# Moving a decoder layer's parameter rows from two queues to a third, and adding two warm-up products

## The chip, the cores and the metric

One Trainium2 chip; the kernel runs on one of its cores. The metric is device time of one execution, in microseconds, median of the runs shown. Smaller is better.

## The reference

One decoder layer on 256 tokens of width 1024. A normalised input `h` goes through one wide projection; two branches (a recurrent mixer and block attention) use its columns, are gated, merged and projected back; then a gated MLP with a short convolution follows.

```python
h = rms_norm(x, norm1_g)                       # x: 256 x 1024
proj = h @ w_in                                # w_in: 1024 x 5408
z = proj[..., :1824]                           # recurrent branch
z = z + rwkv_mu * (shift_right(z) - z)         # per-channel mixing
y_a = rwkv7_time_mix(z, w_decay_up, decay_bias, w_aaa_up, aaa_bias, w_gate_up,
                     k_k, k_a, r_k, ln_g, ln_b)
y_b = moba_attention(rope(q), rope(k), v)      # rope reads `positions`
x = x + (sigmoid(ga) * (y_a @ w_branch_a) + sigmoid(gb) * (y_b @ w_branch_b)) @ w_out
x = x + conv_ffn(rms_norm(x, norm2_g), w_ffn_up, ffn_conv_w, ffn_conv_b, w_ffn_down)
```

What the change touches are the small per-channel vectors: `rwkv_mu`, `decay_bias`, `aaa_bias`, `k_k`, `k_a`, `r_k`, `ln_g`, `ln_b`, and `positions`. None of them is over 8 KB.

## The kernel before, in words

**Products.** Every large product is made in three parts, to keep float32 accuracy with a faster number type: a weight block of 512 KB (`raw`) is fetched, ScalarE (ACT) rounds it to `whi`, VectorE (DVE) takes the rest, `wlo = raw - whi`, and TensorE (PE) multiplies `whi` with the high and the low half of the input (`hh`, `hl`) and `wlo` with the high half. 124 blocks go through these steps; a ring of four `raw` buffers, and four more at the start, let the transfers run ahead.

**The start.** `first_steps()` is written out by hand, engine by engine (a manual schedule: each engine takes its instructions in the order of the code). It holds what happens before the first ordinary block:
- PE first multiplies a tile of ones with itself (`keep_warm`, 8 products of 128x512 in bf16), whose results nobody reads.
- `turn(t, k)` transposes the 16 pieces of `x` on PE (`L427`): first four of the second token half, then the row of `norm1_g` (`p0`, `L438`), then the eight of the first half (`xn`, already scaled by DVE), then the last four.
- ACT and DVE make `hh` (`high`, `L446`) and `hl` (`low`, `L449`) of them.
- `first(0, ..)` and `first(1, ..)` are the products of the first two weight blocks (`L489`), 24 each, into the bank `idle`. Between them stands `params_turned()` (`L149`): PE transposes `p1`, a tile of 43 rows in which all the small vectors of the recurrent branch stand one below the other. DVE then copies the result (`L153`). `p1` is filled by nine small transfers.
- Behind the second block come the transposition of the second half's scale (`L508`) and 32 products with the narrow columns `wtr` (`L515`). Then the ordinary blocks begin (`L304`, `L306`, `L309`).

**The queues.** Transfers are issued by SP (the sync queue), by ACT, and by POOL (GpSimd); each engine issues in its own order. `loads` is a list of the small transfers in this order: the nine rows of `p1`, two of `wdu`, then `wgu`, four of `wgt`, two of `gqk`, `posi` (the positions), three of `p2`. `first_steps()` takes them from the list: ACT issues the first two (`rwkv_mu`, 14 rows and one), SP the two of `wdu`, POOL the other seven rows of `p1` and `posi`.

**Completion counters.** The tile layer gives each transfer of SP and ACT one of eight counters, in rotation, in the order of the code. A transfer that takes a counter in use waits on its queue until the earlier transfer of that counter has landed, and with it waits all that stands behind it on that queue. POOL's transfers have counters of their own. Such waits stand as `DMAHW0` to `DMAHW7` in the lists below.

Of the kernel before, what the change touches and what calls it, by code (L numbers as in the profile page):

```python
# [36 lines left out]
def body(tc, x, positions, norm1_g, w_in, rwkv_mu, w_decay_up, decay_bias, w_aaa_up,  # L37
         aaa_bias, w_gate_up, k_k, k_a, r_k, ln_g, ln_b, q_norm_g, k_norm_g, w_branch_a,
         w_branch_b, w_out, norm2_g, w_up, conv_w, conv_b, w_down, out):
    nc = tc.nc  # L40
    act, dve, pool, pe = nc.scalar, nc.vector, nc.gpsimd, nc.tensor
    ctx = ExitStack()
    with ctx:
# [128 lines left out]
        loads, at_ = [], 0  # L172
# [19 lines left out]
        loads += [(p2[0:66], conv_w[0].rearrange("w (n c) -> (w n) c", c=128)), (p2[66:88], rows(conv_b, 22)),  # L192
                  (p2[88:96], rows(norm2_g, 8))]

        def small_loads(n):
            for _ in range(n):
                nc.gpsimd.dma_start(*loads.pop(0))

        last_exp, last_tanh = [], []
        trig = cst.tile([128, 2, 2, HALF], F32, name="trig")  # L200
        rot = cst.tile([128, 2, 2, 2, 2, HALF], F32, name="rot")
# [43 lines left out]
        def load_next(first=False, early=False):  # L245
            if skipped[0]:
                skipped[0] -= 1
            elif queue:
                ap = queue.pop(0)
                k, c = ap.shape[1], ap.shape[2]  # L250
                raw = b4("raw", (128, 1024)) if early else wp.tile([128, 1024], F32, name="raw", tag="raw", bufs=NRAW)
                rv = raw[:, :k * c].rearrange("p (k c) -> p k c", k=k)
                for ks in ((slice(0, 2), slice(2, 4)) if first else (slice(0, k),)):
                    nc.sync.dma_start(rv[:, ks], ap[:, ks])
                raws.append((raw, k, c))
# [120 lines left out]
        wtr = b2("wtr", [128, 8, 32])  # L376

        def first_steps():
            for _ in range(2):
                nc.scalar.dma_start(*loads.pop(0))  # L380
            for i in range(2 * NRAW):
                load_next(i == 0, early=i >= NRAW)
                if i == 2:
                    nc.sync.dma_start(wtr, win[:, :, 1792:1824])
                if i == 3:
                    for _ in range(2):
                        nc.sync.dma_start(*loads.pop(7))
            skipped[0] = NRAW
            dve.memset(ones, 1.0)
            dve.memset(eps1[:, 0:1], NORM_EPS)  # L390
# [3 lines left out]
            def keep_warm(n):  # L394
                for _ in range(n):
                    pe.matmul(p, ones[:, 0:128], ones, start=True, stop=True)

            keep_warm(8)
            pool.iota(jp, pattern=[[1, 128]], base=0, channel_multiplier=-1)
            pool.tensor_scalar(ident, jp, 0.0, None, op0=OP.is_equal)  # L400
            for q in range(2):
                pool.iota(jl[64 * q:64 * q + 64], pattern=[[0, 2], [1, 64]], base=0, channel_multiplier=-1)
            small_loads(7)
            nc.gpsimd.dma_start(*loads.pop(7))
            act.activation(warm, eps1[:, 0:1], AF.Sqrt)
            ss = sb.tile([128, 2, 2], F32, name="ss1")
            bk = [b("xt") for b in (chp, chp, chp, atp, atp, acc, acc)]
# [17 lines left out]
            def turn(t, k):  # L425
                src = x_sb[t][:, k * 128:k * 128 + 128] if t else xn[k // 4][:, k % 4 * 128:k % 4 * 128 + 128]
                pe.transpose(at(k)[:, t * 128:t * 128 + 128], src, ident)  # L427
# [9 lines left out]
            pt = bk[5][:, 256:264]  # L437
            pe.transpose(pt, p0, ident[:8, :8])  # L438
            dve.tensor_copy(par[:, 0:8], pt)
            for k in (0, 1, 2, 3, 4, 6, 7, 5):  # L440
                turn(0, k)
            for k in (4, 6, 7, 5):
# [2 lines left out]
            def high(k):  # L445
                act.activation(hh[:, k], at(k), AF.Copy, scale=col(G1 + k))  # L446
# [17 lines left out]

            for cs in quarters:
                pool.tensor_copy(w[0][1][:, cs], w[0][0][:, cs])
            for k in (0, 1, 2, 3, 4, 6, 7, 5):
                high(k)
            for cs in halves_:
# [61 lines left out]
        with tc.manual_schedule(engines={E.PE, E.Activation, E.DVE, E.Pool}):  # L531
            xwa, xg, tls = first_steps()
# [825 lines left out]
        for j in range(11):  # L1358
# [20 lines left out]
            for m in range(2):  # L1379
                n = 2 * j + m  # L1380
# [68 lines left out]
```

## Time and profile before

| what | value |
|---|---|
| median of 3 runs | 404.61 us (404.5 to 404.91) |
| the profiled execution | 404.9 us, its span 403.1 us |
| PE busy | 398.0 us, 99% of the span |
| ACT, DVE, POOL busy | 234.7, 321.8, 44.4 us |
| DMA | 70.36 MB, mean 175 GB/s |

The span goes from the first to the last instruction that the profiler saw; 1.8 us of the execution lie around it. PE, ACT, DVE, POOL are the compute engines, PEld is PE's weight load, SP issues transfers. A row of the timeline gives start and duration in us, engine, line, operation, output and inputs with their shapes, the count, and in brackets how long the engine had been idle before and what ended that.

### The profile page before, as it was taken

The page shows a single profiled execution, that of the slowest core. Times are in us where ns is not written, and L with a number is a line of the kernel's source. Part 1 is how long each engine was busy: PE and PEld are TensorE (multiplying, and loading weights), DVE is VectorE, ACT ScalarE, POOL GpSimd, SP SyncE. Part 2 cuts the span into 40 slices and gives each one's busy share as a digit, 9 for nine tenths or more (in the row PEclk, how much of TensorE's full clock was granted, in tenths as well). Part 3 has the DMA queues.
Part 4 walks back from the last instruction along what each step waited for, and adds up shares of the span by engine and source line. Part 5 has one row for each costly group of instructions (what it writes and reads, how often), then busy time and mean ns, then how long its engine had stood idle before and what let it go on. Part 6 is the DMA issues. An engine that isn't in the chain of part 4 may idle for free.

```text
span 403.1 us, 8318 instructions
## 1 busy us (share of the span) xinstructions
PE 398.0 (99%) x3282; PEld 347.9 (86%) x3282; DVE 321.8 (80%) x554; ACT 234.7 (58%) x396; POOL 44.4 (11%) x76
## 2 busy tenths in 40 slices
PE   8999999999999999999999999999999999999996
PEld 5899899888899898999888888888888888888885
DVE  4798999989667897688876897977869779687694
ACT  6899766366555795454564764545546446355450
POOL 7600505213410011100000000000000000000000
PEclk9999999999999999999999999999999999999999
DMA  7983556746844335536664657565665665656612
GB/s 246 299 269 82 138 157 210 205 132 146 224 124 142 106 88 155 167 123 206 201 179 141 210 167 232 165 206 182 198 202 167 209 193 171 209 180 198 195 54 106
DMA packets 60194, 70.36 MB, mean 175 GB/s; under 512 B 7608, under 2 KB 50506, under 8 KB 60154
## 3 DMA queue, kind: packets, MB, share of 16 engines
q1 hardware_dynamic: 59222, 69.40, 57.0%
q0 software_dynamic: 880, 0.41, 0.6%
q8 instruction: 26, 0.43, 0.5%
q14 instruction: 14, 0.11, 0.1%
q10 hardware_dynamic: 52, 0.01, 0.0%
HBM read 68.37 MB, written 1.44 MB: 173 GB/s over the span
## 4 chain that ended last, share of the span: by engine, by line
PE 98%; DMA 1%; SPq 0%; DVE 0%; issue 0%
PE acc L1330 20%; PE acc L1335 10%; PE acc L304 9%; PE acc L306 8%; PE acc L309 8%; PE acc L325 5%; PE acc L329 5%; PE acc L326 5%; PE f L1352 5%; PE f L1350 5%; PE f L1354 5%; PE idle L489 2%; PE pgr L715 1%; PE xt L427 1%; DMA x<-in_x_dram 1%; PE ppt L1155 1%
## 5 line engine op out<-in xcount | busy, mean ns | idle before, releaser
L266 ACT CAST whi<-raw 128x1024 fp32r<-128x1024 f32 x122 | 127.8, 1051 | 111.6 <-PE acc L1330 41.2
L276 DVE TENSOR_TENSOR wlo<-raw,whi 128x1024 fp32r<-128x1024 f32 x122 | 148.3, 1218 | 37.0 <-PE acc L1335 14.0
L1330 PE MATMUL acc<-hx,whi 128*128 128x512 f32 x352 | 89.5, 395 | 0.0
L1330 PEld LDWEIGHTS acc<-hx,whi 128*128 128x128 f32 x352 | 63.4, 188 | 12.4
L304 PE MATMUL acc<-hx,whi 128*128 128x256 f32 x224 | 56.3, 287 | 0.0
L306 PE MATMUL acc<-hx,whi 128*128 128x256 f32 x224 | 54.1, 278 | 0.0
L1335 PEld LDWEIGHTS acc<-hx,wlo 128*128 128x128 f32 x352 | 46.8, 188 | 4.0
L1335 PE MATMUL acc<-hx,wlo 128*128 128x256 f32 x352 | 47.3, 277 | 0.0
L304 PEld LDWEIGHTS acc<-hx,whi 128*128 128x128 f32 x224 | 42.1, 188 | 2.5 <-issue 1.4
L306 PEld LDWEIGHTS acc<-hx,whi 128*128 128x128 f32 x224 | 42.1, 188 | 0.1
L309 PE MATMUL acc<-hx,wlo 128*128 128x256 f32 x224 | 34.6, 276 | 0.0
L1352 PE MATMUL f<-whi,hb 128*128 128x512 f32 x80 | 31.2, 390 | 0.0
L1354 PE MATMUL f<-wlo,hb 128*128 128x512 f32 x80 | 31.2, 390 | 0.0
L1350 PE MATMUL f<-whi,hb 128*128 128x512 f32 x80 | 31.2, 389 | 0.0
L309 PEld LDWEIGHTS acc<-hx,wlo 128*128 128x128 f32 x224 | 29.6, 188 | 0.0
L1340 DVE TENSOR_REDUCE an<-acc 128x256 f32<-128x512 f32 x22 | 14.2, 686 | 9.4 <-PE acc L1335 9.3
L325 PE MATMUL acc<-whi,hx 128*128 128x512 f32 x48 | 19.4, 405 | 0.0
L326 PE MATMUL acc<-whi,hx 128*128 128x512 f32 x48 | 18.8, 391 | 0.0
L1354 PEld LDWEIGHTS f<-wlo,hb 128*128 128x128 f32 x80 | 15.0, 188 | 3.2
L1352 PEld LDWEIGHTS f<-whi,hb 128*128 128x128 f32 x80 | 15.0, 188 | 2.8
L1350 PEld LDWEIGHTS f<-whi,hb 128*128 128x128 f32 x80 | 15.0, 188 | 2.8
L329 PE MATMUL acc<-wlo,hx 128*128 128x512 f32 x48 | 14.9, 392 | 0.0
(341 smaller groups left out, 635.1 us busy)
## 6 DMA issues: line engine op xcount, KB each, us to landing
raw<-in_w_ffn_up_dram SPq DMA_DIRECT2D x44, 512.0 KB, 4.4
raw<-in_w_in_dram SPq DMA_DIRECT2D x41, 512.0 KB, 4.1
raw<-in_w_ffn_down_dram SPq DMA_DIRECT2D x22, 512.0 KB, 3.3
raw<-in_w_out_dram SPq DMA_DIRECT2D x8, 512.0 KB, 3.9
x<-in_x_dram SPq DMA_DIRECT2D x8, 256.0 KB, 4.2
raw<-in_w_branch_b_dram SPq DMA_DIRECT2D x4, 512.0 KB, 4.6
raw<-in_w_branch_a_dram SPq DMA_DIRECT2D x4, 512.0 KB, 3.5
out_dram<-o SPq DMA_DIRECT2D x3, 256.0 KB
```

Source lines behind the costliest of these rows:

```text
L266: act.copy(hi[:, :k * c], raw[:, :k * c])
L276: eng.tensor_tensor(lo[:, :n], raw[:, :n], hi[:, :n].bitcast(F32), op=OP.subtract)
L304: pe.matmul(om, wh[:, k, ms], xh[:, k0 + k], start=k0 + k + m == 0, stop=False, skip_group_check=True)
L306: pe.matmul(om, wh[:, k, ms], xl[:, k0 + k], start=False, stop=False, skip_group_check=True)
L309: pe.matmul(om, wl[:, k, ms], xh[:, k0 + k], start=False, stop=k0 + k == nk - 1 and m == n - 1, skip_group_check=True)
L325: pe.matmul(ps_[t], xh[:, K, ts], wh[:, k], start=K == 0, stop=False)
L326: pe.matmul(ps_[t], xl[:, K, ts], wh[:, k], start=False, stop=False)
L1330: pe.matmul(ps_[m], wh[:, k, m * 128:m * 128 + 128], hx[:, k0 + k].rearrange("p a s -> p (a s)"), start=k0 + k == 0, stop=False, skip_grou ...
L1335: pe.matmul(ps_[m][:, 0:S], wl[:, k, m * 128:m * 128 + 128], hh[:, k0 + k], start=False, stop=k0 + k == 7, skip_group_check=True)
L1350: pe.matmul(fin[f], hb[:, 0, i, ts], wh[:, 0, cs], start=st, stop=False, skip_group_check=f == 3)
L1352: pe.matmul(fin[f], hb[:, 1, i, ts], wh[:, 0, cs], start=False, stop=False, skip_group_check=f == 3)
L1354: pe.matmul(fin[f], hb[:, 0, i, ts], wl[:, 0, cs], start=False, stop=False, skip_group_check=f == 3)
```

## The change

All nine rows of `p1` are issued by SP, behind the third weight block and ahead of `wtr`; `posi` is issued by POOL later, behind its four rounding copies of the first weight block; there is one more `keep_warm` product at the start, and one behind the transposition of `p0`.

```diff
-        def small_loads(n):
-            for _ in range(n):
-                nc.gpsimd.dma_start(*loads.pop(0))
...
         def first_steps():
-            for _ in range(2):
-                nc.scalar.dma_start(*loads.pop(0))
             for i in range(2 * NRAW):
                 load_next(i == 0, early=i >= NRAW)
                 if i == 2:
+                    for _ in range(9):
+                        nc.sync.dma_start(*loads.pop(0))
                     nc.sync.dma_start(wtr, win[:, :, 1792:1824])
                 if i == 3:
                     for _ in range(2):
-                        nc.sync.dma_start(*loads.pop(7))
+                        nc.sync.dma_start(*loads.pop(0))
...
-            keep_warm(8)
+            keep_warm(9)
...
-            small_loads(7)
-            nc.gpsimd.dma_start(*loads.pop(7))
...
             dve.tensor_copy(par[:, 0:8], pt)
+            keep_warm(1)
...
                 pool.tensor_copy(w[0][1][:, cs], w[0][0][:, cs])
+            nc.gpsimd.dma_start(*loads.pop(7))
```

SP's list before, from the second half of the first weight block on (`raw` are weight blocks, the first in two halves; `128x2x256` is half a block):

```order
L254 DMA raw<-in_w_in_dram 128x2x256 [waits DMAHW0_49]
L254 DMA raw<-in_w_in_dram 128x4x256 [waits DMAHW1_49]
L254 DMA raw<-in_w_in_dram 128x4x256 [waits DMAHW2_49]
L384 DMA wtr<-in_w_in_dram 128x8x32 [waits DMAHW3_49]
L254 DMA raw<-in_w_in_dram 128x4x256 [waits DMAHW4_49]
L387 DMA wdu<-in_w_decay_up_dram 64x512 [waits DMAHW5_49]
L387 DMA wdu<-in_w_aaa_up_dram 64x512 [waits DMAHW6_49]
L254 DMA raw<-in_w_in_dram 128x4x256 [waits DMAHW7_49]
```

SP's list now, from the third weight block to the fourth (`p` is `p1`):

```order
L250 DMA raw<-in_w_in_dram 128x4x256 [waits DMAHW0_49]
L379 DMA p_70<-in_rwkv_mu_dram 14x128 [waits DMAHW1_49]
L379 DMA p_70<-in_rwkv_mu_dram 1x4x32 [waits DMAHW2_49]
L379 DMA p_70<-in_decay_bias_dram 4x128 [waits DMAHW3_49]
L379 DMA p_70<-in_aaa_bias_dram 4x128 [waits DMAHW4_49]
L379 DMA p_70<-in_rwkv_k_k_dram 4x128 [waits DMAHW5_49]
L379 DMA p_70<-in_rwkv_k_a_dram 4x128 [waits DMAHW6_49]
L379 DMA p_70<-in_rwkv_r_k_dram 4x128 [waits DMAHW7_49]
L379 DMA p_70<-in_rwkv_ln_g_dram 4x128 [waits DMAHW0_49]
L379 DMA p_70<-in_rwkv_ln_b_dram 4x128 [waits DMAHW1_49]
L380 DMA wtr<-in_w_in_dram 128x8x32 [waits DMAHW2_49]
L250 DMA raw<-in_w_in_dram 128x4x256 [waits DMAHW3_49]
```

The nine rows stand between the third block and `wtr`, and since ACT issues only `p0` now, the counters have moved: 0 is held by `p0` and then by the third block, 1 to 4 by the four pieces of `x`, 5 and 6 by the halves of the first block, 7 by the second block. So the row of `r_k` waits for the second block to land, that of `ln_g` for the third, and that of `ln_b` for the first row of `rwkv_mu`. `wtr`, the fourth block and all behind them come after the last row.

On PE, the stretch from the first transpositions to the first weight block, now:

```order
L421 MATMUL xt<-ident,x 128x128 x4
L432 MATMUL xt<-ident,p_69 128x8
L392 LDWEIGHTS ones
L392 MATMUL idle<-ones 128x512
L421 MATMUL xt<-ident,xn_168 128x128 x4
L421 MATMUL xt<-ident,xn_169 128x128 x4
```

The pair of `ones` is new there; before, the transpositions of `xn` followed that of `p0` (`p_69`) at once. The transposition of `p1` keeps its place between the first and the second weight block on PE, and waits for all nine rows. Line numbers of the new kernel are 4 to 6 lower than before from line 195 on. Apart from these places the order on PE, DVE, ACT and POOL is the same as before; on SP one of the four small `wgt` transfers goes ahead of a later weight block instead of behind it.

## The prediction

> **What bounds the kernel.** First the page: busy times, then the chain that ended last.
>
> ```profile
> PE 398.0 (99%) x3282; PEld 347.9 (86%) x3282; DVE 321.8 (80%) x554; ACT 234.7 (58%) x396; POOL 44.4 (11%) x76
> PE 98%; DMA 1%; SPq 0%; DVE 0%; issue 0%
> ```
>
> PE is busy almost without a break, and 98% of the chain lies on it. So what PE loses or gains at the start it keeps: little later slack takes it back. Everything that the change touches is used in the first 25 us, so PE's timeline there comes next.
>
> ```profile
> 1.46 3.60 PE L396 MATMUL idle<-ones 128*128 128x512 bf16 x8 [1.46 <-DVE eps L391]
> 5.50 1.09 PE L427 MATMUL xt<-ident,x 128*128 128x128 f32 x4 [0.45 <-DMA x<-in_x_dram]
> 6.52 0.27 PE L438 MATMUL xt<-ident,p 8*128 8x8 f32 x1
> 6.72 1.97 PE L427 MATMUL xt<-ident,xn 128*128 128x128 f32 x8
> 8.48 1.06 PE L427 MATMUL xt<-ident,x 128*128 128x128 f32 x4
> 9.20 2.86 PE L489 MATMUL idle<-hx,whi 128*128 128x256 f32 x16
> 11.89 1.07 PE L489 MATMUL idle<-hx,wlo 128*128 128x256 f32 x8
> 12.89 0.26 PE L149 MATMUL pt<-ident,p 43*128 43x43 f32 x1
> 13.08 2.10 PE L489 MATMUL idle<-hx,whi 128*128 128x256 f32 x16
> 15.02 1.07 PE L489 MATMUL idle<-hx,wlo 128*128 128x256 f32 x8
> 15.93 0.27 PE L508 MATMUL pt<-ident,rx 128*128 128x128 f32 x1
> 16.13 1.93 PE L515 MATMUL tl<-hx,wtr 128*32 128x256 f32 x32
> 17.99 0.38 PE L304 MATMUL acc<-hx,whi 128*128 128x256 f32 x1
> ```
>
> PE takes these in this order. The point to watch is L149 at 12.89, the transposition of `p1`: 24 products of the first block stand ahead of it, 24 of the second behind it. If `p1` is late, PE stands. Next, PE's pace: the same product, first and second block (columns of durations: minimum, median, maximum in ns).
>
> ```profile
> L489 PE MATMUL idle<-hx,whi x7: 392/415/562, 9.2 to 10.6; 128*128 128x256 f32 x7
> L489 PE MATMUL idle<-hx,whi x16: 276/276/384, 13.1 to 14.9; 128*128 128x256 f32 x16
> ```
>
> The median falls from 415 to 276 ns, though the granted clock stands at 1.00 in every stretch (third number from the end in the rows of stretches below): until about 10.7 PE ran slowly. The warm-up products aim at that.
>
> **The rows of `p1`: what they leave.** POOL's last row and its landing (last number of the second line, us after issue), and an idle ACT:
>
> ```profile
> 5.51 0.52 POOL L197 DMA_DIRECT2D p<-in_rwkv_ln_b_dram  x1
> ...
> p<-in_rwkv_ln_b_dram POOLq DMA_DIRECT2D x1, 2.0 KB, 6.1
> ...
> 1.39 1.06 ACTq L380 DMA_DIRECT2D p<-in_rwkv_mu_dram  x2
> ...
> 8.11 1.43 POOL L466 CAST whi<-raw 128x256 fp32r<-128x256 f32 x4 [1.31 <-DMA raw<-in_w_in_dram]
> ```
>
> Today `p1` is complete at 5.51 + 6.1 = 11.6, ahead of 12.89. POOL gains its issue time, but then waits for the first weight block until 8.11 as today; ACT gains 1.06, but PE's first transposition waits for `x` until 5.50 whatever ACT does. Both gains I cost at nothing. `posi` moves into POOL's gap behind its copies (9.5 to 11.2) and is needed at 22.3 by DVE: nothing.
>
> **The rows on SP: what they meet.** SP's timeline, the landing of two weight blocks, and SP's own waits:
>
> ```profile
> 3.83 0.47 SPq L254 DMA_DIRECT2D raw<-in_w_in_dram  x1
> raw<-in_w_in_dram SPq DMA_DIRECT2D x1, 512.0 KB, 6.4
> ...
> 4.89 1.21 SPq L384 DMA_DIRECT2D wtr<-in_w_in_dram  x1
> 6.14 2.81 SPq L254 DMA_DIRECT2D raw<-in_w_in_dram  x1
> ...
> 12.26 0.51 SPq L254 DMA_DIRECT2D raw<-in_w_in_dram  x1
> raw<-in_w_in_dram SPq DMA_DIRECT2D x1, 512.0 KB, 8.1
> 20.32 0.32 SPq L1224 DMA_DIRECT2D wgt<-in_w_gate_up_dram  x1
> ...
> SPq L1224 <- DMA raw<-in_w_in_dram: 2.8, 3, 1.9
> ```
>
> The block issued at 12.26 lands at 12.26 + 8.1 = 20.3; the small `wgt`, eight transfers later on its counter, is issued at 20.32. The last line names it: SP waited 2.8 us in three such places. So the counters bind. In the new order the row of `r_k` waits for the second block, 3.83 + 6.4 = 10.2. That of `ln_g` waits for the third block, one block further in the stream. How long a block takes:
>
> ```profile
> 4.00:6.00 2.00, 1.55 (x6) 0.68 (x5) 0.41 (x3) 1.94 (x6) 2.00 (x4) 1.00 0.80 245
> 6.00:8.00 2.00, 2.00 (x10) 1.65 (x9) 1.36 (x4) 1.05 (x5) 0.80 (x2) 1.00 0.91 274
> 8.00:10.00 2.00, 2.00 (x12) 2.00 (x11) 2.00 (x5) 1.86 (x6) 1.43 (x4) 1.00 1.07 370
> ...
> 12.46 1.03 ACT L266 CAST whi<-raw 128x1024 fp32r<-128x1024 f32 x1
> ```
>
> 524 KB at the 370 GB/s of 8 to 10 us (last column) take 1.4: the third block lands at 11.6. It cannot be later than today's 12.46, when ACT rounds it without a wait. The low end: if the eight POOL transfers held the stream back and 4 to 8 us ran at 330 instead of 260 GB/s, 0.28 MB or 0.75 us, would be won: 10.85. Then `ln_g` takes SP about 0.35 (`wgt` above: 0.32), and `ln_b` is issued at 12.0. From issue to landing, with nothing ahead of it, by the nearest rows:
>
> ```profile
> x<-in_x_dram SPq DMA_DIRECT2D x1, 256.0 KB, 2.6
> ...
> out_dram<-o SPq DMA_DIRECT2D x2, 128.0 KB, 1.9
> ...
> X<-d SPq DMA_DIRECT2D x8, 16.0 KB, 2.7
> ```
>
> 256 KB cost 0.7 of streaming at that rate, 128 KB cost 0.35, so the fixed part is 1.5 to 1.9, and at most 2.7. I take 1.8, since `ln_b` has 2 KB and the stream is empty by then. `p1` is complete at 13.8; the bounds are 10.85 + 0.4 + 1.5 = 12.75 and 12.5 + 0.4 + 2.7 = 15.6. The page "DMA: Bandwidth & Descriptors" of the Trainium skill (Latency and other measured facts) speaks for the change: first byte about 0.6 us on a hardware queue, 1 us on GpSimd's. An estimate by that page alone, with its fixed 2 us per transfer, counted from the end of the third block's issue at 4.9 with nine issues of 0.35, would have `p1` at 10.0; this trace's wait at 20.32 is what that count leaves out.
>
> **The sum.** L149 moves from 12.89 to 13.85, +0.95. Behind the stall all inputs of the second block lie ready: from L149 to the first ordinary block pass 17.99 - 12.89 = 5.1 us today, and some 0.2 of it is pauses (of the 16 products from 13.08 on, one takes 384 ns instead of 276: 0.1; between L508 at 15.93 and L515 at 16.13 another 0.1). Net +0.75. The profiled execution took 404.9, 403.1 in its span (the rows' times count from its start) and 1.8 around it, 0.3 above the median of 404.61; the shift goes onto the median: 404.61 + 0.75 = 405.3, rounded down, since later pauses may take back a little.
>
> The two products cost nothing in this account. The ninth ends before `x` is there: the first eight start 0.43 apart (8 in 3.60), and PE is idle for 0.45 before 5.50. The one behind `p0` holds the transpositions of `xn`, and ACT's `high` behind them, back by at most 0.43 - 0.1 = 0.3, which the wait for `p1` covers (PE is through with the first block by 13.2 at the latest). Uncovered, it would cost that 0.3.
>
> **What comes late next.** `wtr` and the fourth block are issued only after `ln_b`:
>
> ```profile
> 15.18 1.05 ACT L266 CAST whi<-raw 128x1024 fp32r<-128x1024 f32 x1 [0.18 <-DMA raw<-in_w_in_dram]
> ...
> 17.09 0.47 ACT L372 ACTIVATE xwa<-idle,omm 128x256 f32<-128x256 f32 x1 [0.85 <-DVE idle L369]
> ```
>
> Today the fourth block lands at 15.18. Now: `ln_b` at 12.0, `wtr` at 12.4 for up to 1.2, the block at 13.6, landing 3.3 later (256 KB in 2.6, and 0.7 more), at 16.9. ACT rounds it, 1.05, ahead of L372, which moves from 17.09 to 17.85. 16.9 + 1.05 = 17.95: just hidden.
>
> **The rivals.** *The weight blocks become the wait (slower).* If `wtr`'s stream delays the block by its own 1 us, or the third block lands as late as today, ACT's L372 comes 1 us later, and with it the inputs that PE needs at 20 us: 404.61 + 0.75 + 1.0 = 406.3. It decides from 16.8 for the landing. For it speaks how close the sum above is; against it that PE has blocks two and three in store. I give it 0.20.
>
> *Full pace early, rows in time (faster).* With PE's two gaps filled (0.45 before 5.50, and around 6.5), PE may reach full pace some 3 us earlier. Then the first block ends when DVE's `wlo` does:
>
> ```profile
> 9.32 1.36 DVE L463 TENSOR_TENSOR wlo<-raw,whi 128x512 fp32r<-128x512 f32 x2
> ...
> 12.24 0.78 DVE L463 TENSOR_TENSOR wlo<-raw,whi 128x512 fp32r<-128x512 f32 x1
> ```
>
> That is 10.68, plus 0.3 for the later `high`, plus half of 1.07: 11.5 for L149, 1.4 earlier, and `wlo` of the second block (13.0) doesn't stop it: 404.61 - 1.4 = 403.2. But each 0.1 us that `p1` lands behind 11.5 takes 0.1 away; the break-even is a landing at 12.9 (13.1 with the 0.2 above). At the low bound of 12.75 it gives 404.4. Chance 0.12. The Trainium skill states the rule in "TensorE: Matmul & The Clock Gate", Part 1: the gate opens after a busy window of about 3.4 us; this trace shows a change near 10.7, 9 us after PE's first product, and one window earlier would be 7.3. Part 4 of the page speaks against it: transpositions do not count as busy, and they fill 5.5 to 9.1 here.
>
> *Pace falls back (slower).* PE would stand from 11.5 to 13.85; if that halved its pace, the next 24 products would take up to 50% more (415 against 276 ns), 3.0 + 1.5: about 407. Chance 0.05, as nothing in this trace shows a pause that did it.
>
> *The rows come in time, the pace stays.* Then only the 0.3 of the product behind `p0` is left: 404.9. Chance 0.10.
>
> **How the numbers follow.** The forecast has 0.53. A difference under 0.2%, 0.8 us, is about what a measurement cannot tell from none. The forecast, 405.3 (its own range 404.4 to 406.4), lies just inside it, with two fifths of its chance beyond. Slower: 0.4 x 0.53 + 0.20 + 0.05 = 0.46; faster: most of 0.12, 0.09; same: the rest, 0.45. The range runs from 404.0, inside the faster rival, to 406.9, above the late weight blocks.
>
> **What would show it.** In the new profile L149 should start between 13.2 and 14.6, with an idle PE ahead of it released by the DMA of `p`; SP should wait ahead of the rows of `r_k` and `ln_g`; the first ordinary block should start near 18.7. L149 at 12 or earlier, or no idle PE ahead of it, refutes the forecast; ACT waiting over 0.5 us for `raw` behind 16 us shows the first rival; L489 at 276 ns before 9 us shows that the warm-up did what the second takes for granted.

## The result and the profile after

The changed kernel takes 407.79 us (median; 407.17 to 408.79) against 404.56 for the kernel before on the same chip: ratio 1.009, 95% interval 1.0076 to 1.0105. It is 3.2 us slower, where 0.7 was forecast, and lies above the range. The execution profiled below took 407.17, with a span of 405.4. Medians and ratios below leave out four far slower executions on record, one of e6 (2224.61 us) and three of the kernel before (439 to 2222 us).

First the page of the changed kernel: busy times, then the chain that ended last.

```profile
PE 398.7 (98%) x3284; PEld 347.0 (86%) x3284; DVE 321.4 (79%) x554; ACT 235.3 (58%) x396; POOL 41.0 (10%) x69
PE 90%; DMA 3%; ACT 3%; SPq 1%; DVE 0%; issue 0%; ACTq 0%
```

PE is as busy as before. But 7% of the chain now lies on DMA, ACT and SP's queue, which before held 1%. (These shares are a hint, no measure: in e8, the same kernel profiled again, PE holds 96%.) PE's timeline at the start, as shown of before:

```profile
1.46 4.02 PE L392 MATMUL idle<-ones 128*128 128x512 bf16 x9 [1.46 <-DVE eps L387]
5.53 1.09 PE L421 MATMUL xt<-ident,x 128*128 128x128 f32 x4
...
6.76 0.61 PE L392 MATMUL idle<-ones 128*128 128x512 bf16 x1
...
8.44 2.13 PE L485 MATMUL idle<-hx,whi 128*128 128x256 f32 x16
10.41 1.26 PE L485 MATMUL idle<-hx,wlo 128*128 128x256 f32 x8
12.87 0.23 PE L149 MATMUL pt<-ident,p 43*128 43x43 f32 x1 [1.21 <-DMA p<-in_rwkv_ln_b_dram]
13.03 2.10 PE L485 MATMUL idle<-hx,whi 128*128 128x256 f32 x16
...
17.94 0.38 PE L300 MATMUL acc<-hx,whi 128*128 128x256 f32 x1
```

Two things are to be seen. The first 24 products end 1.3 us earlier than before (11.67 against 12.96), since PE is at full pace already. And PE then stands 1.21 us for the last row of `p1`. Both cancel: L149 starts at 12.87 (12.89 before), the first ordinary block at 17.94 (17.99). In this execution nothing is lost up to 18 us. SP's timeline shows where the rows went:

```profile
9.65 0.25 SPq L379 DMA_DIRECT2D p<-in_rwkv_r_k_dram  x1
11.05 0.25 SPq L379 DMA_DIRECT2D p<-in_rwkv_ln_g_dram  x1
11.35 0.29 SPq L379 DMA_DIRECT2D p<-in_rwkv_ln_b_dram  x1
11.69 0.40 SPq L380 DMA_DIRECT2D wtr<-in_w_in_dram  x1
12.13 0.57 SPq L250 DMA_DIRECT2D raw<-in_w_in_dram  x1
```

SP's own waits between 4 and 17 us, then the stretches of 2 us (DMA share and GB/s in the last two columns), the changed kernel first and the kernel before below it:

```profile
SPq L379 <- DMA raw<-in_w_in_dram: 3.4, 4, 1.4
```

```profile
10.00:12.00 2.00, 1.67 (x13) 1.40 (x12) 2.00 (x6) 2.00 (x6) 0.85 (x1) 1.00 0.18 34
12.00:14.00 2.00, 1.13 (x9) 1.11 (x10) 1.93 (x10) 1.95 (x5) 1.87 (x5) 1.00 0.61 87
```

```profile
10.00:12.00 2.00, 2.00 (x15) 2.00 (x15) 2.00 (x7) 2.00 (x5) 0.83 (x1) 1.00 1.23 250
12.00:14.00 2.00, 2.00 (x18) 1.82 (x16) 1.93 (x8) 1.95 (x5) 1.88 (x5) 1.00 1.13 295
```

SP stood 3.4 us at four of the rows. All blocks that it had issued landed meanwhile (the third at 11.04), and the fourth is issued only at 12.13 (6.14 before). So the weight stream has a hole: 34 and 87 GB/s, where the kernel before moved 250 and 295. I call this **the hole**. ACT meets it, in order:

```profile
17.00 1.05 ACT L262 CAST whi<-raw 128x1024 fp32r<-128x1024 f32 x1 [2.02 <-DMA raw<-in_w_in_dram]
17.95 0.47 ACT L368 ACTIVATE xwa<-idle,omm 128x256 f32<-128x256 f32 x1
...
20.63 1.05 ACT L262 CAST whi<-raw 128x1024 fp32r<-128x1024 f32 x1 [0.87 <-DMA raw<-in_w_in_dram]
```

It waits 2.02 us for the fourth block and 0.87 for the fifth. PE pays near 35 to 41 us; its waits there (weight loads of PE), of which the profile shown of before has none:

```profile
PEld pss L640 <- ACT sq L629: 0.7, 2, 0.5
...
PEld acc L305 <- DVE wlo L272: 0.3, 1, 0.3
```

Against before, PE is 0.37 late at 35 us and 1.63 at 41, and keeps 1.53 to its last product. The rest of the span's 2.3 lies behind that product: 0.74, to which e11, e13 and e14 belong.

### The profile page after: what moved, and what is told of

Its sections match the earlier page's. It is cut to its first block, busy times and chain, and to the rows that moved or that the text cites. A ratio compares the mean times of both kernels' runs of the same rounds, so it can differ in the third digit from the quotient of the medians.

```text
span 405.4 us, 8313 instructions
## 1 busy us (share of the span) xinstructions
PE 398.7 (98%) x3284; PEld 347.0 (86%) x3284; DVE 321.4 (79%) x554; ACT 235.3 (58%) x396; POOL 41.0 (10%) x69
## 3 DMA queue, kind: packets, MB, share of 16 engines
HBM read 68.37 MB, written 1.44 MB: 172 GB/s over the span
## 4 chain that ended last, share of the span: by engine, by line
PE 90%; DMA 3%; ACT 3%; SPq 1%; DVE 0%; issue 0%; ACTq 0%
PE acc L1326 20%; PE acc L1331 10%; PE acc L300 7%; PE acc L305 7%; PE acc L302 7%; PE acc L321 5%; PE acc L325 5%; PE acc L322 5%; PE f L1348 4%; PE f L1346 4%; PE f L1350 4%; DMA raw<-in_w_in_dram 3%; ACT whi L262 1%; PE pgr L711 1%; PE ppt L1151 1%; PE ps L1123 1%
```

## The experiments

Three theories were on record. **H**: the hole makes ACT late, and PE pays. **P**: the late `p1`, which stops PE at L149, is the cost. **W**: the two warm-up products cost the time. Ratios are to the kernel before on the same chip; e1 to e4, e5 to e8, e9 to e12, and e13 and e14 each shared one.

| run | time us | ratio | 95% interval |
|---|---|---|---|
| e1 warm-up products alone | 404.14 | 0.9988 | 0.9968 to 1.0008 |
| e2 rows on SP alone | 408.18 | 1.0085 | 1.0056 to 1.0114 |
| e3 spare rows on SP | 408.51 | 1.0094 | 1.0061 to 1.0128 |
| e4 last row late on POOL | 406.84 | 1.0065 | 1.0038 to 1.0092 |
| e5 rows divided | 404.92 | 1.0024 | 1.0011 to 1.0038 |
| e6 fourth block first | 409.7 | 1.0148 | 1.0123 to 1.0172 |
| e7 before, again | 404.5 | one run | |
| e8 after, again | 407.75 | one run | |
| e9 after, L149 later | 408.01 | 1.0099 | 1.0078 to 1.0121 |
| e10 divided, L149 later | 403.96 | 0.9999 | 0.9988 to 1.0010 |
| e11 spare rows on POOL | 407.47 | 1.0085 | 1.0068 to 1.0102 |
| e12 warm-up, L149 later | 403.77 | 0.9997 | 0.9987 to 1.0008 |
| e13 longer ACT program | 408.49 | 1.0096 | 1.0078 to 1.0114 |
| e14 longer DVE program | 412.13 | 1.0194 | 1.0178 to 1.0211 |

**e1, the warm-up products alone.** On the kernel before:

```diff
-            keep_warm(8)
+            keep_warm(9)
...
             dve.tensor_copy(par[:, 0:8], pt)
+            keep_warm(1)
```

> The kernel before with the two warm-up products alone; all rows stay where they were (ACT and POOL). Theory H (hole: the rows on SP hold the fourth and fifth weight block back by 1.8 to 3.2 us, ACT's work in order becomes 1.66 us late, PE pays for it near 39 us): no hole, p1 complete near 11.6, PE at full pace from about 7.3, L149 near 11.7; the 1.2 us stay with PE: 403.4 (402.9 to 404.0). Theory P (late p1: the 1.21 us that PE stood ahead of L149 is the cost): the same, 403.4. Theory W (the two products cost the time): 406.5 or more. If ACT, not PE, sets the pace behind 20 us, the early start is worth nothing: 404.6.

W falls: no cost. L149 stood at 11.57, as expected, but of the 1.2 us nothing measurable is left. In its profile PE is still 1.17 ahead of the profiled before at 39 us, and loses 0.75 near 102, in part to this (PE's timeline):

```profile
101.42 0.70 PE L882 MATMUL pp<-X,G 32*32 32x16 f32 x62 [0.44 <-DMA X<-d]
```

e1 to e4 all have such a wait (0.2 to 1.6), e5 to e8 none: the 16 transfers of `X` took 3.6 to 4.5 us to land here (median), 2.1 to 2.9 there. Of the later runs e13 has one (1.1). Why is open, so PE's times behind 102 us are not compared between these groups. Another wait that takes an early start back is seen in e7.

**e2, the rows on SP alone.** The changed kernel with `keep_warm(8)` and without `keep_warm(1)`.

> The changed kernel without the two added products: rows on SP, eight warm-up products. Theory H: the hole is there (the fourth block lands near 17.0, the fifth near 20.5) and ACT is late as in the changed kernel: 407.5 (406.8 to 408.5). Theory P: PE ends the first block at 12.9, p1 lands at 12.7, so nothing is waited for: 404.6 to 405.0. Theory W: 404.6.

As H has it and neither P nor W. P's premise did not hold, however: PE was at full pace early without the added products (the first 24 products ended at 12.04) and stood at L149 as well. PE's timeline:

```profile
13.75 0.23 PE L149 MATMUL pt<-ident,p 43*128 43x43 f32 x1 [1.72 <-DMA p<-in_rwkv_ln_b_dram]
...
21.47 0.67 PE L590 MATMUL fold<-tls,fold 128*128 128x256 f32 x2 [0.97 <-DVE tls L519]
```

So e2 rules out W but can't part H from P.

**e3, the hole without the late `p1`.** e1, with copies of the nine rows on SP into a tile that nothing reads:

```diff
...
                 if i == 2:
+                    for o, r in spare:
+                        nc.sync.dma_start(o, r)
                     nc.sync.dma_start(wtr, win[:, :, 1792:1824])
```

> The two warm-up products, the rows of p1 on ACT and POOL as before, and besides a copy of all nine rows on SP at the place of the change, into a tile that nothing reads: the hole in the weight stream without the late p1. Theory H: L149 near 11.7 without a wait, the fourth block near 17.0, ACT waiting for it; 407.5 (406.8 to 408.5), as slow as the changed kernel. Theory P: 403.4, since p1 is in time. Theory W: 406.5 or more.

P falls. L149 stood at 11.34 without a wait, and the kernel is as slow as the changed one. Its timeline (ACT, then PE):

```profile
17.91 1.04 ACT L266 CAST whi<-raw 128x1024 fp32r<-128x1024 f32 x1 [3.21 <-DMA raw<-in_w_in_dram]
...
20.39 0.67 PE L610 MATMUL fold<-tls,fold 128*128 128x256 f32 x2 [2.31 <-DVE tls L539]
```

The chain reads: fourth block late, ACT's cast late, behind it ACT's `xwa`, behind that DVE's `xwa` and `tls`, and PE waits for `tls` at `fold`. Without the stop at L149 PE comes to `fold` early and waits there instead. At 41 us, ahead of the waits for `X`, PE is 2.8 us later than in e1, which has the same rows at their old place and no hole.

**e4, a late `p1` without the hole.** e1, with POOL's last row behind its first copy:

```diff
-            small_loads(7)
+            small_loads(6)
+            late_row = loads.pop(0)
...
                 pool.tensor_copy(w[0][1][:, cs], w[0][0][:, cs])
+                if cs is quarters[0]:
+                    nc.gpsimd.dma_start(*late_row)
```

> The two warm-up products, rows on ACT and POOL as before, except that POOL issues the last row (ln_b) behind the first of its four copies, at about 8.6: a late p1 without the hole. It should land between 13.0 and 14.7. Theory H: the fourth block lands near 15.2 as before, and PE's stall costs only what L149 starts behind 12.89, one to one: 404.6 for 12.9, 405.6 for 13.9, 406.4 for 14.7. Theory P: as slow as the changed kernel or slower, 407.8 for a landing at 12.7 and 1 us more for each us of delay: 408 to 409.8.

L149 started at 14.33 (the row landed 5.4 us after its issue at 8.56), the fourth block came in time (PE, then ACT):

```profile
14.33 0.23 PE L149 MATMUL pt<-ident,p 43*128 43x43 f32 x1 [1.97 <-DMA raw<-in_w_in_dram]
...
15.37 1.04 ACT L266 CAST whi<-raw 128x1024 fp32r<-128x1024 f32 x1
```

The profile puts the wait down to `raw`, but the row is the transfer that this edit makes late, and in e1 L149 didn't wait. P's 409.1 for this landing (13.98) is far off. H's 406.05 lies just inside the interval (405.9 to 408.1), but the price comes out better from another zero: 14.33 is 2.8 behind the 11.57 of e1, and e4 is 2.7 slower than e1. A late `p1` thus costs by itself, about one to one, but from 11.5 and not from 12.89. Part of the 2.7 is the clock: four of e4's twelve executions have a mean granted clock of 0.996 or less (as e8's, which shows a slow stretch below) and took 408.5 to 410; the other eight have a median of 406.4, 2.3 above e1.

**e5, rows divided.** The changed kernel, with the first four rows on SP and five on POOL:

```diff
-                    for _ in range(9):
+                    for _ in range(4):
                         nc.sync.dma_start(*loads.pop(0))
...
+            for _ in range(5):
+                nc.gpsimd.dma_start(*loads.pop(0))
             act.activation(warm, eps1[:, 0:1], AF.Sqrt)
```

> The changed kernel with its nine rows divided: the first four (which wait for no weight block) stay on SP behind the third block, the five others go back to POOL. Theory H (the counters that r_k and ln_g wait for make the hole): SP issues wtr and the fourth block by about 8.5, no stretch of 2 us with less than 200 GB/s before 16, the fourth block lands by 15.6, L149 near 11.7 without a wait, and the time is that of the kernel with the warm-up products alone: 404.1 (403.4 to 404.8). Rival I (each row on SP costs its issue time ahead of the fourth block, counters or not): four rows of 0.4 to 0.7, some 2 us, keep 2/3 of the delay: the fourth block lands near 16.5 and the time is 406 or more.

No hole: the counters make it, not the issue time of the rows. First the stretch that was empty, then the timeline (SP, PE, ACT):

```profile
10.00:12.00 2.00, 1.09 (x9) 0.81 (x7) 2.00 (x7) 1.97 (x6) 1.39 (x2) 1.00 1.20 243
```

```profile
8.27 0.39 SPq L250 DMA_DIRECT2D raw<-in_w_in_dram  x1
...
12.37 0.23 PE L149 MATMUL pt<-ident,p 43*128 43x43 f32 x1 [1.28 <-DMA p<-in_aaa_bias_dram]
...
14.45 1.05 ACT L262 CAST whi<-raw 128x1024 fp32r<-128x1024 f32 x1
```

Rival I falls: the fourth block is issued 2 us later than before and still in time. But L149 missed its 11.7: the row issued on SP at 6.58 landed only at 12.23, 0.8 us behind the third block, which stood ahead of it. The time is 0.1 above the expected range.

**e6, the fourth block first.** The changed kernel, with `wtr` and the fourth block ahead of the last five rows:

```diff
-                    for _ in range(9):
+                    for _ in range(4):
...
                 if i == 3:
-                    for _ in range(2):
+                    for _ in range(7):
```

> The changed kernel with wtr and the fourth block issued ahead of the last five rows, all rows on SP. k_k now waits for the second block, k_a for the third. Theory H: the fourth block lands by 15.5, p1 lands later than in the changed kernel, near 13.5, so that L149 starts some 0.6 behind 12.89; the fifth block is still late (20.5). If the fourth block is what costs: 404.6 + 0.6 = 405.2 (404.6 to 405.9). If the fifth block costs as much as the fourth: 407 to 408, as the changed kernel.

Missed by 4.5 us. The fourth block was in time (cast at 14.36). But `ln_b`, issued at 12.62 behind that block, landed at 14.85, not near 13.5: PE stood 3.96 us, until 15.21, and then ran slowly. L149, then the stretches (PE's busy time is the second number, the granted clock third from the end):

```profile
15.21 0.23 PE L149 MATMUL pt<-ident,p 43*128 43x43 f32 x1 [3.96 <-DMA wdu<-in_w_decay_up_dram]
...
12.26:15.68 3.42, 0.47 (x3) 0.45 (x4) 0.93 (x4) 3.10 (x4) 3.03 (x9) 1.00 0.48 139
15.68:19.09 3.41, 3.41 (x18) 3.41 (x17) 1.46 (x3) 0.00 (x0) 2.00 (x3) 0.50 1.00 317
```

The granted clock was 0.50 for 3.41 us behind the pause. It is the prediction's third rival, at work.

**e7 and e8, both kernels once more**, without an edit.

> The kernel before, unchanged, profiled a second time, for what differs from run to run: the moment of full pace (10.9 in the first profile), and how long the 16 transfers of X near 97 to 102 take to land (2.6 to 2.7 median, PE not waiting). If the two added products open the gate early, this run has slow products until 10.9 again; if the moment is a matter of the run, it may lie anywhere from 5.7 to 10.9. The time: 404.4 +- 0.8.

> The changed kernel, unchanged, profiled a second time: its first profile (407.17) was the fastest of its runs and had PE 1.5 us late at its end, where the medians differ by 3.2. Theory H: the hole in the weight stream and ACT's wait for the fourth block are there again, near 17; the rest should be found as a wait of PE for the DMA of X near 102, which the first profile lacks and the kernels with rows or spare rows on SP show with 1.1 to 1.6 us. The time: 407.8 +- 0.8.

Kernel before, PE and ACT:

```profile
8.29 2.10 PE L489 MATMUL idle<-hx,whi 128*128 128x256 f32 x16 [0.32 <-POOL whi L466]
...
11.52 0.23 PE L149 MATMUL pt<-ident,p 43*128 43x43 f32 x1 [0.18 <-DMA raw<-in_w_in_dram]
...
14.98 1.05 ACT L266 CAST whi<-raw 128x1024 fp32r<-128x1024 f32 x1 [0.16 <-DMA raw<-in_w_in_dram]
15.94 0.47 ACT L372 ACTIVATE xwa<-idle,omm 128x256 f32<-128x256 f32 x1
```

The kernel before, too, is at full pace early, without the added products: 16 products in 2.10 us from 8.29. L149 stands at 11.52, not 12.89, and `xwa` at 15.94, not 17.09. Twelve of the sixteen profiles reach full pace this early (see the last section); the one on which I predicted is among the four that don't. Yet its span is only 0.4 longer (403.1 against 402.7): PE, 1.37 us earlier at L149, is 0.33 earlier behind 39 us, since it waits for ACT there (PE's waits from 30 to 44 us, then a row of ACT):

```profile
PEld pss L644 <- ACT sq L633: 0.7, 2, 0.5
...
20.18 1.05 ACT L266 CAST whi<-raw 128x1024 fp32r<-128x1024 f32 x1 [0.99 <-DMA raw<-in_w_in_dram]
```

ACT was late there because it had waited 0.99 us for the sixth weight block, which landed at 20.10, 2.87 us behind the fifth (1.5 in the first profile of before, in e1 and in e12). This isn't the price of an early start: e1, e10 and e12 are as early at 36 us, have no such wait for ACT, and lose 0.1 to 0.2 there. e1's profile lost its start near 102 instead.

Changed kernel, second profile, PE's stretches and timeline:

```profile
7.66:11.07 3.41, 2.88 (x25) 2.58 (x23) 3.11 (x8) 3.10 (x9) 2.97 (x6) 1.00 0.85 294
11.07:14.49 3.42, 1.60 (x14) 1.38 (x13) 2.93 (x12) 3.31 (x6) 3.23 (x6) 1.00 0.40 56
14.49:17.90 3.41, 3.41 (x19) 3.41 (x18) 0.87 (x3) 1.22 (x3) 2.28 (x8) 0.50 1.04 302
```

```profile
13.48 0.23 PE L149 MATMUL pt<-ident,p 43*128 43x43 f32 x1 [1.82 <-DMA p<-in_rwkv_ln_b_dram]
13.64 3.10 PE L485 MATMUL idle<-hx,whi 128*128 128x256 f32 x16
```

PE stood 1.82 us, was busy for 47% of a stretch, and the clock fell to 0.50 for the next. The hole is there (56 GB/s, ACT waiting 2.18 for the fourth block). The expected wait for `X` near 102 is not: that part of the expectation missed.

**e9, the hole in the changed kernel without the stop.** L149 and DVE's use of it behind the second block:

```diff
             first(0, 1, hh)
-            params_turned()
-            late_params()
...
             first(1, 1, hh)
+            params_turned()
+            late_params()
```

> The changed kernel with the transposition of p1 (L149) and what DVE makes of it moved behind the 24 products of the second block, so that a late p1 no longer stops PE: the hole alone is left, in the changed kernel itself. (The planner then also puts six products of the third block ahead of the products of wtr.) Theory H (the hole costs by itself): no wait and no slow stretch of the clock ahead of L149, but the fourth block still lands near 17, ACT is late, PE waits at fold or at pss: 406.3 to 408. Theory P (only the late p1 costs): 404.4 plus the 0.7 that the changed kernel has more behind PE's last product: 405.1.

H held, at the upper end of its range, and P fell again: `p1` stops nothing, and the time stays. (Behind the wait at `fold` the clock fell to half for 3.41 us, which took another 0.9.) Its timeline:

```profile
13.60 0.26 PE L149 MATMUL pt<-ident,p 43*128 43x43 f32 x1
...
17.87 1.04 ACT L262 CAST whi<-raw 128x1024 fp32r<-128x1024 f32 x1 [3.61 <-DMA raw<-in_w_in_dram]
...
20.34 0.67 PE L591 MATMUL fold<-tls,fold 128*128 128x256 f32 x2 [2.60 <-DVE tls L520]
```

**e10, neither hole nor stop.** e5 with the edit of e9.

> Rows divided (four on SP, five on POOL, so no hole) and L149 behind the second block, so no wait for p1 either. If hole and late p1 are all that the rows on SP cost up to PE's last product: 404.1 to 404.7 (the divided rows had 0.4 more behind the last product). If rows on SP cost in a third way, 404.9 as with the divided rows before, or more.

403.96, the same as before: a little under what was expected. Four rows on SP cost nothing measurable if none of them waits for a block and PE doesn't stop for them. Against e5 (403.96 to 404.92, on two chips) the stop from 11.5 to 12.37 cost some 0.25%, 1 us; in the two profiles PE differs by 0.4 at 41 us.

**e12, the same with all rows at their old place.** e1 with the edit of e9.

> The two warm-up products, the rows of p1 on ACT and POOL as before, and L149 behind the second block: no hole, and p1, which lands at 11.6 just when PE wants it, no longer stops PE. Expected 404.0 (403.4 to 404.6): at best 0.3 below the kernel with the warm-up products alone, since ACT, not PE, sets the pace near 39.

403.77, no measurable difference to before. PE's wait for ACT near 39, which the expectation counts on, isn't in its profile. No version tried beats the kernel before by more than its interval.

**e11, e13, e14, the 0.74 behind PE's last product.** From the start of PE's last product to the end of the span pass 3.48 us in the kernel before, 3.49 in e7, and 4.22 and 4.24 in the changed kernel. In the trace's record of landings, the 16 parts of the last output transfer arrive by 2.56 us behind that start before. Now 15 parts arrive by 2.61 and one at 3.24, and in the two transfers ahead of it one part is late by 0.7 to 0.8. Beside them stands a code load, this row of the DMA queues from 400 us on, which before has no such row there (its load starts 6.9 us ahead of the product's start, this one 1.2 behind):

```profile
q14 instruction: 1, 0.01, 0.4%
```

e11: seven spare rows on POOL behind `late_consts`; e13 and e14: six small instructions more on ACT or DVE, ahead of the feed-forward blocks:

```diff
+            p1x = cst.tile([28, 128], F32, name="p1x")
+            for i, g in enumerate((decay_bias, aaa_bias, k_k, k_a, ln_g, ln_b, ln_g)):
+                nc.gpsimd.dma_start(p1x[4 * i:4 * i + 4], rows(g, 4))
```

```diff
-                    act.activation(warm, eps1[:, 0:1], AF.Gelu)
+                    for _ in range(7):
+                        act.activation(warm, eps1[:, 0:1], AF.Gelu)
```

```diff
+                    spare = cst.tile([128, 1], F32, name="spare")
+                    for _ in range(6):
+                        dve.memset(spare, 0.0)
```

> The changed kernel, and seven spare rows on POOL into a tile that nothing reads, issued near 17 when POOL has little to do: they give POOL's program the length back that the change took. Theory C (the 0.7 behind PE's last product is a code load of 8 KB that now falls among the last output transfers, since POOL's program is shorter): the load lies 6 us or more ahead of the last product again, the last output lands 2.6 instead of 3.25 behind its start, and the time is 0.7 below the changed kernel: 407.0, ratio 1.007. Rival: the tail comes from SP's nine rows (counter order): it stays at 4.2, and the time at 407.8.

> The changed kernel with six more small instructions on ACT, far behind the change (ahead of the last phase, where ACT is half idle). The 0.7 that the changed kernel has more behind PE's last product goes with a code load of 8 KB that starts 1.2 us behind the start of that product, in every kernel in which ACT has 580 instructions and DVE 707, and 6.7 to 6.9 ahead of it where they have 582 and 709 or more. Theory A (the load is of ACT's code): with 586 on ACT it lies ahead of the last product again, the tail is 3.5, and the time 0.7 below the changed kernel: 407.0 (ratio 1.007). If it is DVE's code: no change, 407.8 (1.009).

> The same with six more small instructions on DVE instead of ACT. Theory D (the load is of DVE's code): with 713 on DVE it lies ahead of the last product again, the tail is 3.5, the time 407.0 (ratio 1.007). If it is ACT's code: no change, 407.8 (1.009). If it moves in neither kernel, its cause stays open.

e11 and e13 missed: load at 1.25 and 1.24, tail 4.24 in both. In e14 the load starts 7.1 us ahead of the product again, the last output lands at 2.65, and the tail is 3.63. So it goes with DVE's program, which the change makes two instructions shorter (707 against 709). All sixteen profiles agree: the load starts 1.2 to 1.4 us behind the product's start in the seven with 707, and 6.7 to 7.1 ahead of it in the nine with 709 or more, whatever the counts of ACT, POOL and SP.

The load is not all. In e3, e5 and e10 it comes early and the last output lands at 2.57, as before, and still the tail is 3.92, 3.86 and 3.86. At the end SP waits for its completion counters one after the other, some 0.06 us each. In the kernel before the last output has the last of them; in e5 six more such waits follow it (0.38), in the changed kernel and in e14 one. So of the changed kernel's 0.74, some 0.68 is the late part and 0.06 this order.

As a time e14 shows nothing, though: it took 412.13, since PE fell behind the changed kernel steadily, from 0.8 us at 41 to 5.6 at the end, in steps of some 0.13. The cause of that is open.

## Why the prediction was wrong

**What costs.** e8 against e7: 405.96 - 402.71 = 3.25 us of span, 2.50 up to PE's last product and 0.75 behind it. Up to the last product: L149 is 1.96 later, the slow clock takes it to 3.58 at 18 us, and 1.06 goes back at 39, where e7 waited for ACT behind its late sixth block. In the first profile of after the clock held: against e7 PE is 1.36 late at L149 and 1.9 at 36 us, where ACT's lateness from the hole shows. Nor is the slow clock the main cost: of the six executions of the result, the four with a mean granted clock of 0.999 or 1.000 have a median of 407.5, and the two with 0.995 and 0.996 took 408.8 and 407.9. Hole and stop lie side by side, and how the loss divides between them in the changed kernel differs from one profile to the other; e3 and e9 show that the hole alone makes the kernel this slow, e4 and e5 that the late `p1` alone costs about what L149 starts behind 11.5.

Point by point:

- *PE bounds, what it loses it keeps.* Mostly: from 44 to 95 us PE's lateness stays within 0.03 in e7, e8 and after. But where one weight block is late, ACT's order takes an early start back (1.07 near 39 in e7), and so do the waits for `X`. These belong to single executions.
- *SP's counters.* Held in mechanism and place: `r_k` at 9.65 (10.2 forecast), `ln_g` 11.05 (11.6), `ln_b` 11.35 (12.0).
- *Landing of `ln_b`.* Over-sized: 1.33 us from issue (landing at 12.68; 1.34 in e2, 1.44 in e8), where I took 1.8 and set 1.5 as the least. `p1` was complete 0.07 below my low bound.
- *The sum, L149 from 12.89 to 13.85.* **The failed step.** The mechanism held, PE standing for `ln_b`, but the zero was wrong: L149 measured 12.85 to 13.75 in the six profiles with all rows on SP ahead of it in this order (so the end was forecast 0.1 to 1.0 too late), and the start that the kernel before shows with early full pace, in e7, is 11.5. The loss is 1.4 to 2.2, not 0.95. The row with 415 ns was the state of one execution, and I took it for the kernel. The 0.2 that was to come back behind L149 was 0.03 (5.07 to the first ordinary block, against 5.10).
- *Fourth block "just hidden".* **The second failed step.** The landing came out right by luck, cast at 17.00 (16.9) and L368 at 17.95 (17.95): the block was issued at 12.13, not 13.6, and took 4.85 us to land, not 3.3. The cover was wrong: L372 at 17.09 had waited 0.85 in that slow execution, and stands at 15.94 in e7. 2 us of lateness were open, and the fifth block (cast at 20.63, with 0.87 of wait) I had not costed. The rival that said so had 0.20 and asked for 0.5 us of ACT's wait behind 16; it was 2.0. Its price for that, 1 us, was half of ACT's 2.
- *"Pace falls back", 0.05.* It happened in e6, e8 (the changed kernel itself), e9 and e14, each time behind a stop of PE.
- *The warm-up products cost nothing.* Held (e1). The rival built on their gain asked for products at 276 ns before 9 us as its sign. The sign came (16 products in 2.13 us from 8.44), but e7 has it without the added products (2.10 us from 8.29), so it shows nothing of them; and `p1` came too late for the rival's time.
- *Behind the last product.* Put at nothing without a reason, since the sum ends at the first ordinary block. It measured 0.75, the third step that failed.

## What to carry to other kernels

A small transfer on a queue with rotating completion counters can wait for a large one, and all that stands behind it waits too; what counts is not its own lateness but the hole that it leaves in the stream behind it, so compare the stream's GB/s by stretches before and after. Look at a second profile before building a sum on a start time: here one execution's clock had moved every zero of the first 18 us. And where an engine is shown waiting 0.85 us, that wait is cover only if the engine that it waits for isn't sometimes earlier.

## What the runs showed of the hardware

**The clock.** The column of the granted clock reads 1.00 for every stretch ahead of the trace's first record of it, so the prediction's reading of that column (1.00 while PE ran slowly) says nothing. In the records themselves, full pace begins between 4.2 and 6.2 us in twelve of the sixteen profiles, with or without the added products (e2 5.71, e7 4.76), and at 7.1 to 10.9 in four: 10.86 in the kernel before, and 7.26, 7.40 and 7.11 in after, e10 and e14, which have the products. Counted back in steps of 3413 ns from that moment, PE's busy time in the first stretch that holds over 1.5 us of it was 2.24 to 2.57 us in the four late ones, and 2.74 to 3.41 in the twelve early ones. Busy time alone does not decide, though: the kernel before was busy for 2.97 us of its second stretch too, and full pace came only after the third. So the added products seem to spare one stretch in the case that comes late, and nothing otherwise; with one profile of the late kind without them, this isn't more than likely. The slow periods of e6, e8, e9 and e14 last 3413 ns each and follow stretches in which PE was busy for 0.47, 1.60, 0.93 and 1.71 us; stretches with 1.70 (e3), 1.95 (e11), 2.08 (e4) and 2.20 (after) were followed by none. So in these traces the limit lies near half a stretch. The Trainium skill, "TensorE: Matmul & The Clock Gate", Part 1, describes a free-running window of 3413 ns, and the traces agree (the slow periods, and 10240 = 3 x 3413 ns at full pace in e8). The same page of the Trainium skill, "Why this matters for your kernels", advises against idle gaps of PE above some 3 us between bursts of products. That is too wide here: 1.82 us inside one window was enough (e8), and 1.97 us across an edge (e4) was not.

**Rows behind blocks.** A row of 2 KB on SP landed 1.33 us after its issue with no block under way ahead of it (after), and 5.7 us after it with a block of 512 KB ahead, which itself landed 0.8 us earlier (e5).

**A code load among the outputs.** One of the 16 parts of each transfer around it lands 0.6 to 0.8 us late (after, against e14), and in these sixteen profiles DVE's count of instructions, 707 or at least 709, tells where the load falls.
